# Low parts of split weights: a VectorE subtraction replaced by an accumulating DMA

## The chip, the core and the metric

The kernel runs on one core of one Trainium2 chip. The metric is device time in microseconds (us) of one execution; the time before is the median of three runs. The core has a matrix engine (TensorE; the profile writes PE for its products and PEld for its weight loads), VectorE (DVE), ScalarE (ACT), GpSimd (POOL) and SyncE (SP). Each takes its instructions strictly in its own order and waits on semaphores for the others. DMAs are issued from an engine's queue; before the change every DMA of the kernel is issued by SP.

## The reference

One layer on a sequence of 2048 positions and 1024 channels, all in float32: a LayerNorm, one wide projection, two branches (attention with 16 heads, and a causal convolution of 31 taps), each closed by a gate and a projection, then a gated merge, an output projection, a residual and a LayerNorm.

```python
h = x @ w_in                                     # 2048x1024 by 1024x9216
q, k, v, z_sb, c_val, c_gate, z_cv, g_sb, g_cv = jnp.split(h, SPLIT_POINTS, axis=-1)
o_sb = _stick_breaking_attention(q, k, v)
y_sb = (o_sb * silu(z_sb)) @ w_sb_proj
u = _causal_depthwise_conv(c_val * sigmoid(c_gate), conv_w, conv_b)
y_cv = (silu(_layer_norm(u, conv_ln_g, conv_ln_b)) * silu(z_cv)) @ w_cv_proj
merged = sigmoid(g_sb) * y_sb + sigmoid(g_cv) * y_cv
return _layer_norm(DEEPNORM_ALPHA * x + merged @ w_out, ln_g, ln_b)
```

## The kernel before

**Split products.** Every float32 matrix a is held as two tiles: hi, its value copied into the type float32r, and lo = a - hi. A product of two such matrices is three matmuls: hi by hi, hi by lo and lo by hi. The helper `split` (L112 to L114) makes the two parts: ACT copies the source into hi (L113), then DVE subtracts hi from the source into lo (L114). It serves the weights, the activations, and the attention weights of each head alike, so L113 and L114 stand for all of them in the profile; the tile names tell them apart: `whi`, `wlo` for weights, `xh`, `xl` for activations, `th`, `tl` for attention weights.

**The projection stream.** The projections are cut into blocks of 128 output columns, 176 of them; a block has two chunks of 512 positions, a chunk four pieces, a piece six matmuls of 128x512 (L194), so 24 matmuls a chunk and 48 a block. `load_w` (L141) brings the 1024x128 weights of a block: twice, for half of the contraction each, SP loads 256 KB into `wraw` (L148) and `split` makes `whi` and `wlo`. There are two `wraw` tiles, each of one half, and two pairs `whi`, `wlo`, each of a whole block: a new block's parts can be written when the block before the last one is used up. The load of the next block is emitted in the second piece of a block.

**Pairs.** At both ends of a run of eight blocks, and in a few other places, `pair` (L221) takes two blocks, a and b, crosswise: first chunk of a, first of b, second of a, second of b. So that one chunk's activations can load beside the other's products. Two of the weight loads there have a single chunk, 24 matmuls, between the moment at which their tiles come free and the moment at which they are needed: that of b, and that of the block after the pair.

**The weave.** TensorE's order is the order of emission. The attention (logits L572 and L573, sigmoid on ACT L575, running product on DVE L578 into `nb`, transposes L601, split into `th` and `tl`, product with the values L617) and the projection stream are woven into one list by estimated costs. The other engines' orders are made by the scheduler from priorities. The attention ends about 2660 us after the start; then come the attention branch's projection for the second half, an output projection (L900), the convolution branch's projection, and a last output projection. In these the blocks run without attention beside them.

**GpSimd** does little: some memsets, the power -0.5 and the products for the norms (L124, L119, one column each), and copies of single columns (L322 to L326, L377).

Of the kernel before, what the change touches and what calls it, by code (L numbers as in the profile page):

```python
# [8 lines left out]
F32 = mybir.dt.float32  # L9
F32R = mybir.dt.float32r  # L10
AF = mybir.ActivationFunctionType
ALU = mybir.AluOpType
# [13 lines left out]

# The weave: buffers of weights, the lead of the logits, and distances and paces in pieces of the projection stream.
NBW = 4
# [26 lines left out]
def layer_kernel(ctx: ExitStack, tc, x, w_in, w_sb, w_cv, w_out, vecs, cw, rows, out):  # L55
    """All sequences are reversed in time: row r is position S-1-r, so that a query r reads
    the keys s > r and the stick is broken in the direction of growing s.

    Every float32 product runs as float32r passes over an exact split a = hi + lo.

    The tensor engine runs in the order of emission: two streams, the attention and the
    projections, are woven so that what one waits for is covered by the other."""
    nc = tc.nc
# [28 lines left out]
    def dma(dst, src):  # L92
        """A copy of bytes: float32r has float32's bits."""
        nc.sync.dma_start(out=dst.bitcast(F32) if dst.dtype == F32R else dst,
                          in_=src.bitcast(F32) if src.dtype == F32R else src)
# [20 lines left out]
    def negmean(mr):  # L116
        """-mean * rstd"""
        nm = sm.tile([P, 1], F32, name="nm")
        nc.gpsimd.tensor_scalar(out=nm, in0=mr[:, 0:1], scalar1=mr[:, 1:2], scalar2=-1.0, op0=ALU.mult, op1=ALU.mult)  # L119
        return nm  # L120
# [18 lines left out]

    # -------------------------------------------------------------- projections, in pieces  # L140
    def load_w(src, col):  # L141
        """A block of 128 columns of a weight, [block, partition, kb, column], as hi and lo, contraction on the partitions."""
        hi = wp.tile([P, KB, P], F32R, name="whi", bufs=2)
        lo = wp.tile([P, KB, P], F32R, name="wlo", bufs=2)
        for g in range(2):
            ks = slice(g * 4, g * 4 + 4)
            raw = wp.tile([P, 4, P], F32, name="wraw", bufs=2)
            nc.sync.dma_start(out=raw, in_=src[col // P][:, ks])  # L148
            split(raw, hi[:, ks], lo[:, ks])
        return hi, lo  # L150

    class Fill:
        """The pieces of the projection stream: (cost in us of the tensor engine, emit)."""

# [20 lines left out]
        def parts(self, src, col, xs, use, *by):  # L175
            """A block: the pieces, per chunk, of out^T[col.., chunk] for each (chunk, acts) of xs; use(chunk, psum, ..) takes
            it, with what the loads `by` have brought. Also the item that loads the weights of the next block."""
            b = {"src": (src, col)}
            me = len(self.blocks)
            self.blocks.append(b)  # L180

            def chunk(c, acts):
                box = {}

                def piece(g):
                    if g == 0:
                        self.weights(me)
                        box["ps"] = mm_p.tile([P, CH], F32, name="mm")
                        box["by"] = [load(c) for load in by]
                    wh, wl = b["w"]  # L190
                    xh, xl = acts()
                    for kb in (2 * g, 2 * g + 1):
                        for n, (l, r) in enumerate(((wh, xh), (wh, xl), (wl, xh))):
                            nc.tensor.matmul(box["ps"], lhsT=l[:, kb], rhs=r[kb], start=(kb == 0 and n == 0),  # L194
                                             stop=(kb == KB - 1 and n == 2))
                    if g == 3:
                        with tc.high_priority(offset=500):
                            use(c, box["ps"], *box["by"])
                return [(1.3, lambda g=g: piece(g)) for g in range(4)]

            return [chunk(c, acts) for c, acts in xs], (0, lambda: self.weights(me + 1))
# [19 lines left out]
        def pair(self, one, two, first=(), freed=((), ())):  # L221
            """Two blocks, the first chunk of both before the second of either. The items `first` run beside these
            pieces, freed[n] as the activations of chunk n are used up."""
            (a, na), (b, nb) = self.parts(*one), self.parts(*two)
# [27 lines left out]
    def prep(c):  # L252
        """The normed input of chunk c, transposed and split, into xt[c], in pieces."""
        rows_ = []
# [28 lines left out]
    def xa_tile(to, key):  # L283
        """The next block of a chunk's activations, hi and lo."""
        t = [xa.tile([P, CH], F32R, name=n, bufs=2 * KB) for n in ("xh", "xl")]
        hi, lo = to.setdefault(key, ([], []))
        hi.append(t[0])
        lo.append(t[1])
        return t
# [65 lines left out]
    def even_odd(t):  # L355
        """A row kept as its even and then its odd positions, in the order of the positions."""
        return t.rearrange("p (e n) -> p n e", e=2)

    def block_u(F, m, h):
        """u = c_val * sigmoid(c_gate) of a block of channels."""  # L360
        sg = {}
# [21 lines left out]

    # -------------------------------------------------------------- causal depthwise convolution, norm over channels
    ysum = {}
    convs = []

    def conv(m, h, u):
        """y[r] = sum over d of t[d] u[r+d] + b, with t the taps reversed, on even and odd positions:
        y0 = t0 * (u0 - u1) + (t0 + t1) * u1,  y1 = t1 * (u0+ - u1) + (t0 + t1) * u1."""  # L390
        n = HN + H1
# [38 lines left out]
    def conv_mean(h):  # L430
        """The means over the channels of half h, as items."""
        def mean(c):
# [8 lines left out]
    def conv_ln(c):  # L441
        """The norm over the channels of chunk c, the swish and the gate of the branch, as items."""
        nb = CH // P
# [56 lines left out]

    # -------------------------------------------------------------- attention, in items
    def attention(at, kv, lg_p, pv_p):
        """Summed by parts: with E[r, s] the product of 1 - sigmoid over the keys after r up to s, the weight of s is
        E[r, s-1] - E[r, s], so that o[r] = v[r] + sum over s >= r of E[r, s] (v[s+1] - v[s]), with v[S] = 0."""
        dd = at.tile([P, HALF], F32, name="dd", bufs=1)
# [10 lines left out]
        def head(i, a, h):  # L516
            """The steps of head 2i+a for the queries of half h, each (L items, T/PV items)."""
            k2, v2, qd, ql = {}, {}, {}, {}
# [124 lines left out]
    def weave_attention(steps):  # L643
        """The steps as one list of (cost, emit): the logits run ahead of the transposes, those of the products."""
        ls = []
# [23 lines left out]

    # -------------------------------------------------------------- branch projections, output  # L670
    acts = {}

    def load_acts(key, src, c):
        """The activations of chunk c, split where they land, as items."""
        def load(m):
            hi, lo = xa_tile(acts, key)
            raw = st()
            dma(raw, src[c, m])
            split(raw, hi, lo)
        return [(0, lambda m=m: load(m)) for m in range(KB)]  # L680

    def branch(n, h):
        """A gated branch of the merge for half h: of the attention into pdr, of the convolution into mdr."""
        def gate(m):
# [28 lines left out]
    def run(F, blks, freed):  # L713
        """The blocks of a half, by pairs at both ends so that one chunk's activations load beside the other's products."""
        F.pair(*blks[:2])
# [26 lines left out]
    def newest():  # L742
        """The newest instruction of the vector engine."""
        return next((i for i in reversed(nc.cur_bb.bb.instructions) if i.engine == mybir.EngineType.DVE), None)
# [19 lines left out]

    # -------------------------------------------------------------- the main phase
    with ExitStack() as s2:
# [90 lines left out]

    # -------------------------------------------------------------- the rest
    with ExitStack() as s2:
# [20 lines left out]
        def output(F, c, freed):  # L880
            """The output projection of chunk c, the residual and the post-norm."""
            def unit(j, z, q, g, box):
# [92 lines left out]
```

## Time and profile before

| | |
|---|---|
| median of 3 runs (lowest, highest) | 3039.43 us (3039.3, 3042.27) |
| profiled execution, first to last instruction (its span) | 3036.5 us |
| lies around the span, by the median | 2.9 us |
| PE, PEld, DVE, ACT, POOL busy | 2959.8, 2484.1, 2381.6, 1269.5, 88.3 us |
| DMA moved | 455.92 MB, 16 engines 46.0% busy |
| granted TensorE clock, mean | 0.996 |

The profiled execution has no separate device time on record, only its span. In the profile a row of a timeline gives start, duration, engine, line, operation, output tile <- input tiles, and in brackets the idle time of that engine before it and what ended it. L194 means line 194 of the kernel before. Matmuls overlap in the records: a 128x512 matmul shows 0.39 us, though the next starts about 0.23 us after it.

### The profile page before, as it was taken

What the parts mean: (1) busy time and instruction counts of PE and PEld (TensorE: products, weight loads), DVE (VectorE), ACT (ScalarE), POOL (GpSimd) and SP (SyncE); (2) the same over time, 40 slices, a digit from 0 to 9 for tenths busy, and PEclk for the clock granted to TensorE, in tenths of its full rate; (3) what the DMA queues carried; (4) which work ended last, traced back from release to release, by engine and by line L of the source; (5) the groups of instructions that cost most, each with busy time, mean ns of one, the idle gap of its engine ahead of it and who ended that gap; (6) DMA issues with size and microseconds to landing.
All of it is one profiled execution on the core that took longest, in us unless ns stands there. A gap on an engine that the chain in (4) does not pass through costs nothing.

```text
span 3036.5 us, 41850 instructions
## 1 busy us (share of the span) xinstructions
PE 2959.8 (97%) x15304; PEld 2484.1 (82%) x15304; DVE 2381.6 (78%) x3175; ACT 1269.5 (42%) x2308; POOL 88.3 (3%) x178
## 2 busy tenths in 40 slices
PE   7999999999999999999999999999999999999998
PEld 6888888888887788888888888887888878878886
DVE  5587787777879888788879888879887788856656
ACT  5333333333336344444445444445445455533222
POOL 1000000000000000000000000000000000000000
PEclk9999999999999999999999999999999999999999
DMA  7543443434434533343335344335545666685552
GB/s 269 172 144 112 148 139 117 149 125 130 139 101 140 169 100 110 114 131 123 111 112 189 103 143 141 99 103 175 164 155 161 191 224 191 208 280 197 161 189 78
DMA packets 260221, 455.92 MB, mean 150 GB/s; under 512 B 30384, under 2 KB 55088, under 8 KB 259888
## 3 DMA queue, kind: packets, MB, share of 16 engines
q1 hardware_dynamic: 260016, 453.25, 46.0%
q8 instruction: 120, 1.97, 0.3%
q14 instruction: 85, 0.70, 0.1%
HBM read 292.70 MB, written 160.43 MB: 149 GB/s over the span
## 4 chain that ended last, share of the span: by engine, by line
PE 73%; DVE 11%; issue 10%; DMA 3%; ACT 2%; POOL 1%; SPq 0%; DVEq 0%; POOLq 0%; ACTq 0%
PE mm L194 52%; PE pv L617 7%; PE tp L601 6%; DVE nb L578 3%; PE lg L573 3%; PE lg L572 3%; DVE tl L114 2%; DVE wlo L114 1%; DVE cy L402 1%; PE mo L900 1%; DMA st<-ydq 1%; DMA ydq<-st 1%; DVE xl L114 1%; DVE st L494 0%; DVE st L493 0%
## 5 line engine op out<-in xcount | busy, mean ns | idle before, releaser
L194 PE MATMUL mm<-xh,whi 128*128 128x512 f32 x2816 | 1144.5, 406 | 1.7 <-ACT whi L113 1.5
L194 PE MATMUL mm<-xh,wlo 128*128 128x512 f32 x2816 | 1110.1, 394 | 1.4 <-DVE wlo L114 1.4
L194 PE MATMUL mm<-xl,whi 128*128 128x512 f32 x2816 | 1106.2, 393 | 1.2 <-DVE xl L114 1.2
L194 PEld LDWEIGHTS mm<-xh,wlo 128*128 128x128 f32 x2816 | 530.0, 188 | 120.9 <-DVE wlo L114 1.9
L194 PEld LDWEIGHTS mm<-xl,whi 128*128 128x128 f32 x2816 | 532.9, 189 | 86.8 <-DVE xl L114 2.4
L194 PEld LDWEIGHTS mm<-xh,whi 128*128 128x128 f32 x2816 | 531.5, 189 | 86.4 <-ACT whi L113 1.9
L113 ACT ACTIVATE th<-tp 128x512 fp32r<-128x512 f32 (+1 forms) x576 | 329.4, 572 | 613.9 <-PE tp L601 606.1
L114 DVE TENSOR_TENSOR tl<-tp,th 128x512 fp32r<-128x512 f32 (+1 forms) x576 | 376.5, 654 | 180.1 <-ACT th L113 178.2
L575 ACT ACTIVATE nb<-lg 128x512 f32<-128x512 f32 (+3 forms) x640 | 334.9, 532 | 308.9 <-PE lg L573 299.0
L578 DVE TENSOR_TENSOR_SCAN nb<-nb,dd 128x256 f32<-128x256 f32 (+7 forms) x256 | 345.1, 1350 | 42.2 <-ACT nb L575 41.5
L601 PE MATMUL tp<-ident,nb 128*128 128x128 f32 x2176 | 337.8, 274 | 20.3 <-DVE nb L578 18.2
L578 DVE TENSOR_TENSOR_SCAN nb<-nb,zero 128x1024 f32<-128x1024 f32 x128 | 300.0, 2346 | 36.5 <-ACT nb L575 36.2
L601 PEld LDWEIGHTS tp<-ident,nb 128*128 128x128 f32 x2176 | 263.4, 140 | 77.9 <-DVE nb L578 22.5
L113 ACT ACTIVATE whi<-wraw 128x512 fp32r<-128x512 f32 x352 | 217.6, 629 | 261.1 <-PE mm L194 238.8
L617 PE MATMUL pv<-tl,v 128*128 128x256 f32 (+1 forms) x1152 | 292.1, 282 | 12.2 <-DVE tl L114 11.6
L114 DVE TENSOR_TENSOR wlo<-wraw,whi 128x512 fp32r<-128x512 f32 x352 | 237.4, 682 | 80.0 <-ACT whi L113 52.9
L617 PE MATMUL pv<-th,v 128*128 128x256 f32 (+1 forms) x1152 | 299.5, 281 | 0.0
L572 PE MATMUL lg<-k,qd 128*128 128x512 f32 (+3 forms) x640 | 246.4, 386 | 11.6 <-ACT nb L575 7.0
L617 PEld LDWEIGHTS pv<-tl,v 128*128 128x128 f32 x1152 | 218.1, 189 | 36.4 <-DVE tl L114 17.2
L573 PE MATMUL lg<-k,ql 128*128 128x512 f32 (+3 forms) x640 | 233.7, 366 | 0.0
L617 PEld LDWEIGHTS pv<-th,v 128*128 128x128 f32 x1152 | 217.8, 189 | 18.5 <-issue 0.2
L402 DVE SCALAR_TENSOR_TENSOR cy<-cu,csum,cy 128x512 f32<-128x512 f32 x240 | 178.1, 742 | 4.4 <-ACT cy L398 0.9
(107 smaller groups left out, 2460.0 us busy)
## 6 DMA issues: line engine op xcount, KB each, us to landing
wraw<-in_w_in SPq DMA_DIRECT2D x288, 256.0 KB, 3.2
k<-kdr SPq DMA_DIRECT2D x192, 128.0 KB, 2.9
v<-vdr SPq DMA_DIRECT2D x96, 256.0 KB, 3.5
kdr<-st SPq DMA_DIRECT2D x64, 256.0 KB, 2.1
qdr<-st SPq DMA_DIRECT2D x64, 256.0 KB, 2.2
qd<-qdr SPq DMA_DIRECT2D x128, 128.0 KB, 2.8
vdr<-st SPq DMA_DIRECT2D x64, 256.0 KB, 2.0
xr<-in_x SPq DMA_DIRECT2D x32, 256.0 KB, 3.8
```

Of the source, the lines that this page charges most:

```text
L113: nc.scalar.activation(hi, src, AF.Copy)
L114: nc.vector.tensor_tensor(out=lo, in0=src, in1=hi.bitcast(F32), op=ALU.subtract)
L194: nc.tensor.matmul(box["ps"], lhsT=l[:, kb], rhs=r[kb], start=(kb == 0 and n == 0), stop=(kb == KB - 1 and n == 2))
L402: nc.vector.scalar_tensor_tensor(out=dst, in0=src[:, j:j + HN], scalar=t, in1=first, op0=ALU.mult, op1=ALU.add)
L572: nc.tensor.matmul(lg[:, :w], lhsT=qd[c][:, js], rhs=k2[kc][:, ko:ko + w], start=True, stop=False)
L573: nc.tensor.matmul(lg[:, :w], lhsT=ql[c][:, js], rhs=k2[kc][:, ko:ko + w], start=False, stop=True)
L575: nc.scalar.activation(nb[:, o:o + w], lg[:, :w], AF.Sigmoid, scale=-QS)
L578: nc.vector.tensor_tensor_scan(out=nb[:, :w], data0=nb[:, :w], data1=dd[:, :w] if diag else zero.to_broadcast([P, w]), initial=0.0 if diag ...
L601: nc.tensor.transpose(out=tp[:, at_:at_ + P], in_=tiles[j][:, so:so + P], identity=ident)
L617: nc.tensor.matmul(o[:, :w], lhsT=lv, rhs=tt[:, o0:o0 + w], start=(diag and t == 0 and n == 0 and e == 0), stop=(last and t == nt - 1 and ...
L900: nc.tensor.matmul(ps, lhsT=a[kb][:, js], rhs=b[:, kb, qs], start=(kb == 0 and n == 0), stop=(kb == KB - 1 and n == 2))
```

## The change

In `load_w` alone, the raw weights are still loaded into `wraw` and copied into `whi` by ACT. Then ACT copies `whi` with scale -1 into `wlo`, and a DMA issued by GpSimd reads the same 256 KB of weights from memory once more and adds them to what stands in `wlo`. DVE no longer takes part. The other callers of `split` are as they were. Lines below the change stand two lower than before (L194 becomes L196).

```diff
             raw = wp.tile([P, 4, P], F32, name="wraw", bufs=2)
             nc.sync.dma_start(out=raw, in_=src[col // P][:, ks])
-            split(raw, hi[:, ks], lo[:, ks])
+            nc.scalar.activation(hi[:, ks], raw, AF.Copy)
+            nc.scalar.activation(lo[:, ks], hi[:, ks].bitcast(F32), AF.Copy, scale=-1.0)
+            nc.gpsimd.dma_start(out=lo[:, ks], in_=src[col // P][:, ks].bitcast(F32R), accum_op=ALU.add)
```

It takes 352 instructions from DVE and adds 352 to ACT and 352 DMAs to GpSimd's queue. A `wraw` tile is now free once ACT has read it. The third product of a block on TensorE waits for the DMA instead of DVE; TensorE's order is the same, row by row.

On GpSimd at the start of the program, before: the powers and products of the norm of the input's rows (`mrs`, `nm`), then the single columns of the first value block (`st`, `vnext`).

```order
L124 TENSOR_TENSOR mrs<-mrs,mhalf 128x1
L119 TENSOR_SCALAR nm<-mrs 128x1
L124 TENSOR_TENSOR mrs<-mrs,mhalf 128x1
L119 TENSOR_SCALAR nm<-mrs 128x1
L124 TENSOR_TENSOR mrs<-mrs,mhalf 128x1
L119 TENSOR_SCALAR nm<-mrs 128x1
L124 TENSOR_TENSOR mrs<-mrs,mhalf 128x1
L119 TENSOR_SCALAR nm<-mrs 128x1
L322 TENSOR_SCALAR st<-st 128x1
```

The same place now, with the accumulating DMAs of line 151.

```order
L124 TENSOR_TENSOR mrs<-mrs,mhalf 128x1
L119 TENSOR_SCALAR nm<-mrs 128x1
L151 DMA wlo<-in_w_in 128x512
L124 TENSOR_TENSOR mrs<-mrs,mhalf 128x1
L119 TENSOR_SCALAR nm<-mrs 128x1
L151 DMA wlo<-in_w_in 128x512 x2
L124 TENSOR_TENSOR mrs<-mrs,mhalf 128x1
L119 TENSOR_SCALAR nm<-mrs 128x1
L124 TENSOR_TENSOR mrs<-mrs,mhalf 128x1
L119 TENSOR_SCALAR nm<-mrs 128x1
L151 DMA wlo<-in_w_in 128x512 x5
L324 TENSOR_SCALAR st<-st 128x1
```

The first half of block 0 stands behind the norm of the fifth group of rows, the second half of block 0 and the first of block 1 behind the sixth, the second of block 1 behind the eighth.

On ACT where the attention has ended and the last phase begins, before: the parts of the two blocks of a pair (`whi`), between activations (`xh`) and the output weights (`woh`).

```order
L113 ACTIVATE whi<-wraw 128x512 x2
L113 ACTIVATE xh<-st 128x512 x3
L113 ACTIVATE woh<-raw 128x1024 x3
L113 ACTIVATE xh<-st 128x512 x5
L113 ACTIVATE whi<-wraw 128x512
L113 ACTIVATE xh<-st 128x512
L113 ACTIVATE whi<-wraw 128x512
L113 ACTIVATE xh<-st 128x512 x3
```

The same place now.

```order
L149 ACTIVATE whi<-wraw 128x512 x2
L113 ACTIVATE xh<-st 128x512
L150 ACTIVATE wlo<-whi 128x512
L113 ACTIVATE xh<-st 128x512
L150 ACTIVATE wlo<-whi 128x512
L113 ACTIVATE woh<-raw 128x1024
L113 ACTIVATE xh<-st 128x512
L113 ACTIVATE woh<-raw 128x1024
L149 ACTIVATE whi<-wraw 128x512
L113 ACTIVATE woh<-raw 128x1024
L113 ACTIVATE xh<-st 128x512 x3
L150 ACTIVATE wlo<-whi 128x512
```

The copies of block a of the pair stand together before and have an `xh` between them and each negation now. The first copy of block b has moved ahead of the last `woh` and three `xh`, and its negation stands behind these.

## Prediction

> **What bounds the kernel now.** I read the page first, for the busy times.
>
> ```profile
> span 3036.5 us, 41850 instructions
> PE 2959.8 (97%) x15304; PEld 2484.1 (82%) x15304; DVE 2381.6 (78%) x3175; ACT 1269.5 (42%) x2308; POOL 88.3 (3%) x178
> ```
>
> PE is busy 97% of the span, but matmul records overlap, so this alone doesn't say that PE is at its pace. The timeline of PE does:
>
> ```profile
> 1500.55 0.39 PE L194 MATMUL mm<-xh,whi 128*128 128x512 f32 x1
> 1500.78 0.40 PE L194 MATMUL mm<-xl,whi 128*128 128x512 f32 x1
> 1501.01 0.39 PE L194 MATMUL mm<-xh,wlo 128*128 128x512 f32 x1
> ```
>
> One product starts every 0.23 us, with no gap, in the middle of the weave. TensorE sets the time; what DVE saves is worth only the moments at which TensorE waits for DVE. The waits of TensorE's weight loads name them (total, times, longest):
>
> ```profile
> PEld tp L601 <- DVE nb L578: 22.5, 18, 3.5
> PEld pv L617 <- DVE tl L114: 17.2, 21, 2.2
> PEld tp L275 <- DVE xr L266: 13.1, 4, 12.3
> PEld lg L572 <- ACT nb L575: 10.7, 11, 2.6
> PEld tp L601 <- DVE tl L114: 3.8, 7, 0.8
> PEld mm L194 <- DVE wlo L114: 1.9, 1, 1.9
> ```
>
> The 13.1 us for `xr` are the first transposes of the program, which wait for the input. The other four rows with DVE make 22.5 + 17.2 + 3.8 + 1.9 = 45.4 us: no relief of DVE can bring more, out of 3036.5. The weights' low part itself is waited for once.
>
> **What is removed.** The groups by line price the subtraction and the copy beside it:
>
> ```profile
> L113 ACT ACTIVATE whi<-wraw 128x512 fp32r<-128x512 f32 x352 | 217.6, 629 | 261.1 <-PE mm L194 238.8
> L114 DVE TENSOR_TENSOR wlo<-wraw,whi 128x512 fp32r<-128x512 f32 x352 | 237.4, 682 | 80.0 <-ACT whi L113 52.9
> ```
>
> DVE loses 237.4 us, nearly all of it beside TensorE's work. How tight DVE is, stage by stage (length, then busy time of PE, PEld, DVE, ACT and POOL, clock, DMA share, GB/s):
>
> ```profile
> 60.00:900.00 840.00, 837.82 (x4246) 702.46 (x4245) 641.29 (x895) 305.94 (x592) 28.39 (x54) 1.00 0.42 136
> 1100.00:2300.00 1200.00, 1182.71 (x6364) 999.27 (x6363) 1005.20 (x1251) 529.67 (x981) 17.73 (x26) 1.00 0.41 130
> 2300.00:2680.00 380.00, 360.59 (x1970) 305.92 (x1969) 317.88 (x403) 200.63 (x360) 2.03 (x2) 0.99 0.64 204
> ```
>
> Up to 900 us TensorE loses 2 us in 840: nothing to gain. From 1100 to 2680 DVE is busy 84%. The subtractions are 237.4 / 3036.5 = 8% of the time, so 84% becomes 76%. If waiting in a queue goes as load over idle share, 0.84/0.16 = 5.2 becomes 0.76/0.24 = 3.2, 40% less. On the 43.5 us behind `nb` and `tl` that is 17 us, and the 1.9 us go too. The form of this rule is my assumption; the bounds are 0 and 45.4.
>
> **What is added on ACT.** 352 negations, which no row has; the copy beside them, 629 ns, is the nearest, with a start 0.52 us after the one before where two stand together (whi x2 in 1.16 us, below). That is 220 us, and ACT goes from 42% to 49%. Between 1100 and 2300 us its 530 / 1200 = 44% becomes 51%, load over idle share from 0.8 to 1.05, a third more. On the 10.7 us that TensorE waits for ACT this is 3.5 us. The splits `th`, whose lateness DVE's `tl` inherits, I put at as much again: 7 us. So the balance of the engines is 17 + 2 - 7 = 12 us gained; I take 10.
>
> **What is added as DMA.** 352 transfers of 256 KB more. Nothing issued by POOL, and no accumulation, is in this trace. The rows nearest to it (issue to landing, us), and the slowest kind of POOL operation (ns, minimum/median/maximum):
>
> ```profile
> kdr<-st SPq DMA_DIRECT2D x64, 256.0 KB, 2.1
> wraw<-in_w_in SPq DMA_DIRECT2D x288, 256.0 KB, 3.2
> wraw<-in_w_sb SPq DMA_DIRECT2D x32, 256.0 KB, 4.2
> raw<-in_w_out SPq DMA_DIRECT2D x8, 512.0 KB, 6.0
> L124 POOL TENSOR_TENSOR var<-var,mhalf x4: 1007/1241/1465, 1478.3 to 2571.4; 128x4 f32<-128x4 f32 x4
> ```
>
> From below: a load like any other, 3.2 us. From above: it moves its bytes twice, like the 512 KB load, 6.0, with some of the crowd of the last phase and a POOL operation for the issue, 8 us in all. I take the last phase's plain load and one such operation, 4.2 + 1.2 = 5.4 us from the end of the negation to the landing; call it X. The Trainium skill, "DMA: Bandwidth & Descriptors", section "Anatomy of one DMA — SWDGE (gpsimd) path", fits 2.0 us plus the bytes at 436 GB/s for a DMA from GpSimd, an estimated 2.6 us here; by it the shortfalls of 1.2 us below are gone. The trace's plain loads take longer than that, so I don't lower X.
>
> Does TensorE wait for X? A block's tiles come free one block ahead of its use. With attention woven in, a block lasts some 17 us (3036.5 / 176), and X plus the copies passes unseen. The short places are the pairs, where 24 products at 0.23 us, 5.5 us, are all there is. One in the last phase, on ACT and then PE:
>
> ```profile
> 2866.23 1.16 ACT L113 ACTIVATE whi<-wraw 128x512 fp32r<-128x512 f32 x2 [7.67 <-PE mm L194]
> ...
> 2872.15 0.39 PE L194 MATMUL mm<-xh,wlo 128*128 128x512 f32 x1
> ```
>
> ACT waits for the tile, copies both halves until 2867.39, and the low part is needed at 2872.15. Now the first negation ends at about 2867.9, and 4.2 us are left: X = 5.4 is 1.2 us late. The code has six such places after the attention (a pair at each end of the two runs, less the two loads that the output projection covers). Three are like this one: 3.6 us. At the first, an `xh` stands between copy and negation: 1.2 + 0.5 = 1.7. The other two are later on ACT:
>
> ```profile
> 2671.51 0.43 SPq L148 DMA_DIRECT2D wraw<-in_w_sb  x1
> ...
> 2676.20 0.63 ACT L113 ACTIVATE whi<-wraw 128x512 fp32r<-128x512 f32 x1
> 2690.88 1.14 ACT L113 ACTIVATE whi<-wraw 128x512 fp32r<-128x512 f32 x2
> ...
> 2679.05 0.50 PE L194 MATMUL mm<-xh,wlo 128*128 128x512 f32 x1 [1.43 <-DVE wlo L114]
> 2695.50 0.39 PE L194 MATMUL mm<-xh,wlo 128*128 128x512 f32 x1
> ```
>
> The block of 2695.50: 2690.88 + 1.14 + 0.5 + 5.4 = 2697.9, 2.4 us late. The block of 2679.05 already waits. Its first copy now stands ahead of a `woh` and three `xh`, its negation behind them. If SP loads at 2671.51 as before, the raw weights are there at 2675.7, the copy ends at 2676.2, and 1 + 3 x 0.55 + 0.5 later, at 2679.4, the negation; landing 2684.8, 5.7 us late. If SP, no longer held by DVE, loads 3 us earlier, it is 2.8 us; I take 4.5. The last phase: 3.6 + 1.7 + 2.4 + 4.5 = 12 us. At X = 8 it is 2.6 us more at each of six places, 28 us; at X = 3.2 only the fifth is left, about 2.
>
> **The start.**
>
> ```profile
> 14.82 0.33 SPq L148 DMA_DIRECT2D wraw<-in_w_in  x1
> ...
> 15.23 0.61 ACT L113 ACTIVATE whi<-wraw 128x512 fp32r<-128x512 f32 x1
> 15.75 1.43 ACT L278 ACTIVATE st<-tp,vec 128x512 f32<-128x512 f32 x2
> ...
> 17.44 0.59 POOL L119 TENSOR_SCALAR nm<-mrs 128x1 f32<-128x1 f32 x1
> ...
> 20.87 0.63 PE L194 MATMUL mm<-xh,wlo 128*128 128x512 f32 x1
> ```
>
> Ahead of the `st` of 15.75 ACT now has one negation, two copies and two negations more or less together, of which the second copy needs the third raw load. That load waited for DVE until 14.82 and now waits only for ACT; with 3 to 5 us to land it is there at about 16.5, so `st` comes near 18, 2.3 us later, and TensorE's first product with it. POOL issues the first accumulation behind the `nm` that ends at 18.0; 18.0 + 5.4 = 23.4, against 20.87 + 2.3 = 23.2. The next block's is behind one more norm, which waits for its rows, and adds 1.5; the block after this pair, a short place as above, 1. Start: 2.3 + 0.2 + 1.5 + 1 = 5 us, between 2 and 9.
>
> **Crowding.** 92 MB on 456 MB, a fifth more. In 2300 to 2680 us the DMA engines' 0.64 goes to some 0.75, and the loads of activations there come later: 3 us, between 0 and 8. POOL's single columns for `st` now queue behind accumulations that wait for ACT. POOL had waited long for its inputs there, and a few us hide; nothing.
>
> Sum: 5 + 12 + 3 - 10 = +10 us on the span of 3036.5, 3046.5; with the 2.9 us around it, 3049.5 against the median of 3039.43, 0.33% slower. About 0.2%, 6 us, is what a measurement of this kernel tells from no change.
>
> **The rivals.**
> - *DVE's relief decides (faster).* X stays under the 4.2 us of slack, so the last phase costs 2 us, the start 3, crowding 0, and the queue rule holds in full with little harm from ACT: 5 - 18 = -13, 3026. For it: plain loads take 3.2 us, and DVE is the engine TensorE waits for most. Against: the last phase's loads take 4.2.
> - *A slow accumulation.* X is 8 us or more: start 9, last phase 28, the woven pairs, with some 8 us of lead, 8 more, crowding 7, less 10: +42, 3081. A way to it: each issue on POOL is held by the DVE instruction then running, up to 2.35 us for the longest running products below, so X = 5.4 + 2.35 = 7.75.
>
> ```profile
> L578 DVE TENSOR_TENSOR_SCAN nb<-nb,zero 128x1024 f32<-128x1024 f32 x128 | 300.0, 2346 | 36.5 <-ACT nb L575 36.2
> ```
>
> The Trainium skill, "SBUF — State Buffer", section "SBUF: two separate sides", has this as the "DVE blocks DMA" trap: GpSimd can't write descriptors while DVE holds their shared port in a two-port mode. No run here shows it yet; by the 0.23 us pace of the products it would show only in pairs.
> - *Nothing measurable.* The same terms with X near 4.2: 3 + 6 + 1 - 10 = 0, 3039.
> - *The change not doing what it says* is no rival for DVE, whose rows are gone from the order; but the raw load stays, so it saves no transfer.
>
> **How the numbers follow.** Forecast 0.38 (+6 to +30 us), slow accumulation 0.13, nothing measurable 0.25, relief 0.24. So faster 0.24, same 0.25, slower 0.51. The range leaves out a tenth on each side: 3022, near the relief's largest gain less the unavoidable start, to 3082, the slow accumulation as priced.
>
> **What would show it.** Right: DVE near 2144 us, ACT near 1490; waits of PE for a DMA into `wlo` at the start and at the six places, 1 to 5 us each; `nb` and `tl` waits down by a third. Landings of `wlo` near 5 us from issue. Wrong: landings under 4 us with no wait on `wlo`; or over 8, with waits on `wlo` all over the weave; or `nb` and `tl` waits as large as before or larger, which would say that ACT has taken over DVE's part.

## The result and the profile after

| | before | changed |
|---|---|---|
| median of the runs, us (lowest, highest) | 3040.22 (3039.3, 3042.27), 4 runs | 3123.52 (3120.13, 3127.55), 4 runs |
| ratio, 95% interval | | 1.0276 [1.0263, 1.0289] |
| profiled execution: device time, span | no time, 3036.5 | 3127.55, 3125.8 |
| mean granted TensorE clock | 0.996 | 0.983 |

The changed kernel is 83 us, 2.8%, slower (84 us against the 3039.43 us on record before; below it is called 84). The direction was forecast, the size was not: 10 us forecast, 3082 the upper end. The page of the changed kernel (engines; then the DMA queues, with packets, MB and share of 16 engines):

```profile
span 3125.8 us, 42335 instructions
...
PE 2998.6 (96%) x15304; PEld 2507.3 (80%) x15304; DVE 2183.0 (70%) x2823; ACT 1447.3 (46%) x2660; POOL 389.7 (12%) x530
...
q1 hardware_dynamic: 260016, 453.25, 45.2%
q0 software_dynamic: 50688, 92.30, 17.9%
```

DVE is relieved, ACT loaded, as the change says. The last row is GpSimd's queue: 92 MB take 17.9% of the engines, where SP's 453 MB take 45.2%. Per megabyte that is 0.194% against 0.0997%, twice as much.

The waits of TensorE's weight loads, changed kernel:

```profile
PEld tp L603 <- DVE nb L580: 33.5, 19, 4.4
PEld mm L196 <- DMA wlo<-in_w_sb: 19.3, 5, 7.2
PEld lg L574 <- ACT nb L577: 18.6, 13, 3.8
PEld pv L619 <- DVE tl L114: 18.3, 30, 1.7
...
PEld mm L196 <- DMA wlo<-in_w_cv: 6.7, 2, 3.4
PEld mm L196 <- DMA wlo<-in_w_in: 5.9, 3, 3.0
PEld pv L619 <- ACT th L113: 5.8, 6, 2.7
```

Two things stand in it. TensorE waits for accumulations, 31.9 us in ten waits. And the attention's waits for DVE and ACT, which the relief was to shorten, have grown: `nb` behind DVE from 22.5 to 33.5, behind ACT from 10.7 to 18.6, and `th` from 0.2 to 5.8.

Four stages of it (start and end, length, busy PE, PEld, DVE, ACT, POOL, clock, DMA share, GB/s):

```profile
62.00:930.00 868.00, 861.41 (x4364) 721.18 (x4362) 585.34 (x794) 378.23 (x730) 131.59 (x177) 1.00 0.65 173
...
1100.00:2300.00 1200.00, 1177.67 (x6279) 993.61 (x6278) 913.54 (x1095) 590.95 (x1104) 133.31 (x163) 0.99 0.59 158
2300.00:2730.00 430.00, 395.75 (x2099) 332.51 (x2098) 314.04 (x382) 228.03 (x416) 37.20 (x42) 0.96 0.71 206
2730.00:2780.00 50.00, 38.71 (x135) 30.31 (x136) 15.94 (x21) 17.64 (x27) 5.22 (x6) 0.80 0.84 262
```

From 62 to 930 us TensorE is idle for only 7 us, with as much traffic as anywhere behind the start in the program's first half. Between 1100 and 2300 us it starts 85 products fewer than before in the same time, some 16 us at the pace before. Most of the time is lost after that, in the end of the attention and in the last phase, above all its first pairs, and there the granted clock is 0.96 and 0.80. What the clock does behind a wait, on the timeline of PE:

```profile
2761.24 0.39 PE L196 MATMUL mm<-xl,whi 128*128 128x512 f32 x1
2768.42 0.79 PE L196 MATMUL mm<-xh,wlo 128*128 128x512 f32 x1 [6.79 <-DMA wlo<-in_w_sb]
...
2769.44 0.63 PE L196 MATMUL mm<-xl,whi 128*128 128x512 f32 x1
2769.86 0.63 PE L196 MATMUL mm<-xh,wlo 128*128 128x512 f32 x1
...
2774.40 0.39 PE L196 MATMUL mm<-xl,whi 128*128 128x512 f32 x1
2774.63 0.40 PE L196 MATMUL mm<-xh,wlo 128*128 128x512 f32 x1
```

After the wait of 6.79 us products start 0.43 us apart instead of 0.23, until 2774: 13 of them, 2.6 us more that no wait names. The same stands behind a wait of 2.98 us that ends at 2730.5. The Trainium skill, "TensorE: Matmul & The Clock Gate", section "Part 1: The HAM clock gate", says that idleness puts the clock at half and that activity is judged in windows of 3.4 us; the 5.7 us of slow products here agree with a return after one or two of these.

The landings (KB each, median us from issue), which the prediction had at 5.4 us from the end of the negation:

```profile
wlo<-in_w_in POOLq DMA_DIRECT2D x288, 256.0 KB, 6.2
...
wlo<-in_w_sb POOLq DMA_DIRECT2D x32, 256.0 KB, 7.3
...
wlo<-in_w_cv POOLq DMA_DIRECT2D x32, 256.0 KB, 7.0
```

### The profile page after: what moved, and what is told of

Same layout as the page of the kernel before. It is cut to its first block, busy times and chain, and to the rows that moved or that the text cites. A ratio compares the mean times of both kernels' runs of the same rounds, so it can differ in the third digit from the quotient of the medians.

```text
span 3125.8 us, 42335 instructions
## 1 busy us (share of the span) xinstructions
PE 2998.6 (96%) x15304; PEld 2507.3 (80%) x15304; DVE 2183.0 (70%) x2823; ACT 1447.3 (46%) x2660; POOL 389.7 (12%) x530
## 3 DMA queue, kind: packets, MB, share of 16 engines
q1 hardware_dynamic: 260016, 453.25, 45.2%
q0 software_dynamic: 50688, 92.30, 17.9%
## 5 line engine op out<-in xcount | busy, mean ns | idle before, releaser
L196 PE MATMUL mm<-xh,whi 128*128 128x512 f32 x2816 | 1154.5, 410 | 0.8 <-DVE st L114 0.5
L196 PE MATMUL mm<-xh,wlo 128*128 128x512 f32 x2816 | 1120.1, 398 | 27.4 <-DMA wlo<-in_w_sb 17.2
L196 PE MATMUL mm<-xl,whi 128*128 128x512 f32 x2816 | 1115.7, 396 | 2.2 <-DVE xl L114 2.2
L196 PEld LDWEIGHTS mm<-xh,wlo 128*128 128x128 f32 x2816 | 535.6, 190 | 152.8 <-DMA wlo<-in_w_sb 19.3
L196 PEld LDWEIGHTS mm<-xl,whi 128*128 128x128 f32 x2816 | 538.5, 191 | 90.1 <-DVE xl L114 3.9
L196 PEld LDWEIGHTS mm<-xh,whi 128*128 128x128 f32 x2816 | 537.5, 191 | 86.8 <-DVE st L114 1.0
L151 POOL DMA_DIRECT2D wlo<-in_w_in x288 | 251.1, 891 | 1616.3 <-ACT wlo L150 1265.5
L603 PEld LDWEIGHTS tp<-ident,nb 128*128 128x128 f32 x2176 | 265.9, 141 | 91.5 <-DVE nb L580 33.5
L150 ACT ACTIVATE wlo<-whi 128x512 fp32r<-128x512 f32 x352 | 218.0, 629 | 2.4
```

Of the source, the lines that this page charges most:

```text
L150: nc.scalar.activation(lo[:, ks], hi[:, ks].bitcast(F32), AF.Copy, scale=-1.0)
L151: nc.gpsimd.dma_start(out=lo[:, ks], in_=src[col // P][:, ks].bitcast(F32R), accum_op=ALU.add)
L603: nc.tensor.transpose(out=tp[:, at_:at_ + P], in_=tiles[j][:, so:so + P], identity=ident)
```

## The experiments

Four costs could make the 84 us: less relief than thought, ACT's negations, the new traffic, and the waits for it. The first runs add them one by one. Each time is a median beside its own runs of before (3038.6 to 3040.4).

**Relief alone.**

```diff
             nc.scalar.activation(hi[:, ks], raw, AF.Copy)
-            ...negation, accumulating DMA
-        return hi, lo
+        return hi, hi
```

> The low parts of the weights aren't made at all: neither subtraction, negation nor accumulation; the third product reads the high part in their place. So DVE loses its 352 subtractions and nothing is added. If the relief of DVE is worth what the prediction said (17 to 19 us of waits), 3020 to 3030 us. If it is worth nothing because the attention's waits have another cause, 3037 to 3043.

3025.1 us, ratio 0.9947 [0.9930, 0.9964]: 14 us gained. The relief is real, and this is all there is of it. TensorE's waits behind `nb` and `tl`, to be read against 22.5, 17.2, 10.7 and 3.8 before:

```profile
PEld tp L600 <- DVE nb L577: 20.5, 15, 2.7
PEld pv L616 <- DVE tl L114: 13.8, 22, 1.7
...
PEld lg L571 <- ACT nb L574: 8.4, 12, 1.9
PEld tp L600 <- DVE tl L114: 4.9, 7, 1.9
```

Some 4 us less behind DVE and 2 less behind ACT. Of the 8 us besides, 1.9 are the low part's wait, and some 5 are products that took less time: PE is busy 2955.2 us for the same 15304 products, where it was 2959.8.

**Relief and the negations.**

```diff
             nc.scalar.activation(lo[:, ks], hi[:, ks].bitcast(F32), AF.Copy, scale=-1.0)
-            nc.gpsimd.dma_start(out=lo[:, ks], in_=..., accum_op=ALU.add)
         return hi, lo
```

> The accumulating DMA is left out; the low part is the negated high part that ACT writes. DVE is relieved, ACT has the 352 negations, TensorE waits for no DMA. Theory that ACT's added work makes the attention stage worse: 25 to 45 us over the run with the relief alone. Theory that the extra DMA traffic does it: within 10 us of the run with the relief alone.

3034.9 us, 0.9981 [0.9972, 0.9991]. The negations cost 10 us of the 14, with TensorE's wait for ACT's `nb` up from 8.4 to 12.6. That is less than the theory of ACT needs.

**The negations without the relief.** As the run before, and in the place of the DMA:

```diff
+            nc.vector.tensor_tensor(out=lo[:, ks], in0=raw, in1=lo[:, ks].bitcast(F32), op=ALU.add)
```

> No accumulating DMA: ACT negates, and DVE adds the raw weights to the negation, so DVE has as many operations as before and ACT 352 more. Theory that ACT's added work costs: 25 us or more over before, 3065. Theory that traffic and waits cost, not ACT: within 10 us of before, 3030 to 3050.

3053.0 us, 1.0040 [1.0025, 1.0055], 14 us over before: between the two expectations. ACT's part is 10 to 14 us, whether DVE is relieved or not.

**All the work, but nobody waits for it.**

```diff
-        return hi, lo
+        return hi, hi
```

> All of the change's work is done, negation and accumulating DMA, but the third product reads the high part, so TensorE never waits for an accumulation. The change took 84 us. Theory that waits for the accumulations at the start and in the pairs, with the half clock behind each, make 45 us: about 3078. Theory that the traffic itself is what costs in the attention stage: 30 us or more over the run without the DMA. Theory that ACT does it: within 10 us of the run without the DMA.

3088.0 us, 1.0158 [1.0143, 1.0173]: 53 us over the run without the DMA. The traffic costs more than all else, though TensorE doesn't read what it brings. The last 35 us come when TensorE does read it, as waits and what follows them. So the theory of waits alone (3078) falls short, and that of ACT falls. How it costs, first in the landings of the others, without the DMA and then with it:

```profile
k<-kdr SPq DMA_DIRECT2D x192, 128.0 KB, 2.8
...
wraw<-in_w_sb SPq DMA_DIRECT2D x32, 256.0 KB, 4.1
st<-asb SPq DMA_DIRECT2D x32, 256.0 KB, 3.5
```

```profile
k<-kdr SPq DMA_DIRECT2D x192, 128.0 KB, 3.7
...
wraw<-in_w_sb SPq DMA_DIRECT2D x32, 256.0 KB, 5.7
st<-asb SPq DMA_DIRECT2D x32, 256.0 KB, 4.6
```

These land 0.9 to 1.6 us later, though not all do: the raw weights of `in_w_in` go from 3.1 to 3.4 us. Then in the waits of ACT, without and with:

```profile
ACT st L459 <- DMA ydq<-st: 33.3, 18, 4.7
...
ACT xh L113 <- DMA st<-asb: 4.0, 6, 1.2
```

```profile
ACT st L460 <- DMA ydq<-st: 55.5, 19, 5.5
...
ACT xh L113 <- DMA st<-asb: 17.6, 15, 4.0
```

All waits of ACT for transfers together go from 116 to 195 us. ACT takes its instructions in order: while it waits for a late transfer of `st`, what stands behind it waits too, the attention's sigmoids `nb` and splits `th` among it, then DVE's running products and splits, and TensorE behind both. That path is pieced together from the waits at its two ends; TensorE's end, without and with:

```profile
PEld tp L602 <- DVE nb L579: 21.1, 17, 3.0
...
PEld lg L573 <- ACT nb L576: 12.6, 12, 3.6
PEld pv L618 <- DVE tl L114: 10.2, 17, 1.6
```

```profile
PEld tp L603 <- DVE nb L580: 32.5, 18, 3.5
PEld pv L619 <- DVE tl L114: 20.6, 28, 1.8
PEld lg L574 <- ACT nb L577: 17.7, 15, 3.8
```

These three rows grow by 27 us. The stage in which convolution norms and activations are loaded beside the attention, without and with:

```profile
2300.00:2680.00 380.00, 360.99 (x1976) 304.73 (x1975) 297.93 (x368) 219.90 (x399) 2.03 (x2) 1.00 0.64 205
```

```profile
2300.00:2680.00 380.00, 347.60 (x1847) 291.12 (x1846) 281.49 (x339) 203.84 (x374) 31.82 (x36) 0.96 0.71 207
```

In the same 380 us TensorE now starts 1847 products instead of 1976, 7% fewer, with a granted clock of 0.96 instead of 1.00. The bytes per second are about the same, 207 against 205, with the accumulations among them.

**A sixteenth of the bytes.** Is it the bytes, or the 352 issues on GpSimd and what queues behind them?

```diff
-            nc.gpsimd.dma_start(out=lo[:, ks], in_=src[col // P][:, ks]...
+            nc.gpsimd.dma_start(out=lo[:, 4 * g, :32], in_=src[col // P][:, 4 * g, :32]...
```

> As the run whose accumulation is unread, but each accumulating DMA moves 128 bytes a partition, a sixteenth, so the low part is left negated but for that piece, and the third product reads the high part. Count, order and waits of GpSimd's queue stay. Without the DMA the kernel took 3035, with it 3088. Theory that the bytes crowd the other transfers: near 3035 to 3045. Theory that the issues on GpSimd, or what queues behind them, cost: 3075 or more.

3034.9 us, 0.9988 [0.9978, 0.9998], the time without any DMA, though the third product reads the high part here too. So as many issues and packets cost nothing; the bytes do.

```profile
q0 software_dynamic: 50688, 5.79, 3.4%
```

**A plain copy of the same bytes.**

```diff
-            nc.gpsimd.dma_start(out=lo[:, ks], in_=src[col // P][:, ks].bitcast(F32R), accum_op=ALU.add)
+            nc.gpsimd.dma_start(out=lo[:, ks].bitcast(F32), in_=src[col // P][:, ks])
```

> As the run whose accumulation is unread, but GpSimd's DMA writes the raw weights over the negation in place of adding; the third product reads the high part. Same bytes from memory, no reading of the destination. In the changed kernel an accumulated megabyte takes the DMA engines twice as long as any other (17.9% of them for 92 MB, 45.2% for 453). Theory that the engines' time is what crowds: the cost over 3035 halves, 3055 to 3065, and the landing falls from 6.1 to about 4.5 us. Theory that bytes from memory crowd: 3080 or more.

3058.2 us, 1.0064 [1.0047, 1.0081]: 23 us over the run without the DMA, against 53 for the accumulation.

```profile
q0 software_dynamic: 28160, 92.30, 9.8%
...
wlo<-in_w_in POOLq DMA_DIRECT2D x288, 256.0 KB, 4.5
```

The share of the engines is 9.8%, against 18.4% for the accumulation in the unread run, and the cost falls with it, from 53 to 23 us, while the bytes from memory are the same. The median landings of the other transfers hardly tell the two apart (`k` 3.5 us, `st` from `asb` 4.5, `wraw` of `in_w_sb` 5.2); ACT's waits for transfers do, 160 us in all against 195, where it was 116 without the DMA and 128 with a sixteenth of the bytes. The copy differs from the accumulation in its type as well, float32 where that has float32r, so which of the two makes the price is not shown.

**Added from SBUF.**

```diff
-            nc.gpsimd.dma_start(out=lo[:, ks], in_=src[col // P][:, ks].bitcast(F32R), accum_op=ALU.add)
+            nc.gpsimd.dma_start(out=lo[:, ks], in_=raw.bitcast(F32R), accum_op=ALU.add)
```

> As the run whose accumulation is unread (3088), but the DMA adds the raw weights from the tile in SBUF into which SP has loaded them, so 92 MB less is read from memory; the third product reads the high part. Theory that the DMA engines' time crowds the other transfers: 3070 or more, with about the same share of the engines. Theory that reads from memory crowd: 3060 or less. The raw tile is held until the accumulation lands, which may cost some us of its own.

3108.4 us, 1.0231 [1.0215, 1.0247]. With 92 MB less read from memory and nearly the same share of the engines, 17.5%, it is 20 us slower than the run that reads memory. That is the first theory's side of the expectation, but the waits of SP say that the run doesn't test it:

```profile
SPq L148 <- DMA wlo<-wraw: 909.4, 321, 14.0
```

SP, in order too, stands 909 us waiting for raw tiles that the accumulation holds, where it had stood 276 us for ACT, so other loads are issued late. Once issued they land sooner than in the unread run, `wraw` of `in_w_sb` after 3.1 us instead of 5.7 and `k` after 3.2 instead of 3.7. So this run decides neither way; that the reads from memory alone don't set the cost rests on the plain copy.

**Halves.** The waits for accumulations, by giving them more lead and changing nothing else:

```diff
-        hi = wp.tile([P, KB, P], F32R, name="whi", bufs=2)
-        lo = wp.tile([P, KB, P], F32R, name="wlo", bufs=2)
+        hi, lo = [], []
         for g in range(2):
+            hi.append(wp.tile([P, 4, P], F32R, name=f"whi{g}", bufs=2))
+            lo.append(wp.tile([P, 4, P], F32R, name=f"wlo{g}", bufs=2))
...
```

> The changed kernel, with the parts of a block held in two tiles of half the contraction each, in the same space. A half comes free 12 products earlier or is needed 12 later, so a pair leaves 8 us in place of 5.5. Nothing else is changed. Theory that the 35 us between the unread run and the changed kernel are waits for the accumulations with too short a lead: the waits on it after the start vanish, 3090 to 3100. If these 35 us come of something else: 3115 or more.

3085.3 us, 1.0149 [1.0134, 1.0164]: 38 us less than the changed kernel, more than the 24 to 34 expected. The waits for accumulations are not gone, as they were expected to be after the start, but less than half:

```profile
PEld mm L197 <- DMA wlo<-in_w_sb: 9.3, 3, 6.3
...
PEld mm L197 <- DMA wlo<-in_w_in: 3.3, 3, 1.9
...
PEld mm L197 <- DMA wlo<-in_w_cv: 1.8, 3, 1.0
```

Between the two profiled executions PE has 25 us less idle time and 22 us less busy time for the same products. So the pace comes back with the waits gone.

**Halves in the kernel before**, the control.

> The kernel before, with VectorE's subtraction, and the parts of a block in two tiles of half the contraction each: the control for the run of the changed kernel with halves, which came out 38 us faster than the changed kernel. Theory that halves only take away waits for the accumulations: within 6 us of before, which waits for a low part once. If halves help by themselves, for instance because ACT's copies wait less for tiles: 3030 or less, and that much of the 38 us is not the accumulation's.

3033.0 us, 0.9984 [0.9976, 0.9993], 6 us less than before: at the border of the first expectation. So some 32 of the 38 us are the accumulation's. This kernel computes the whole layer and is, by a little, faster than the kernel before.

**The subtraction on GpSimd**, another way to the relief:

```diff
+            nc.gpsimd.tensor_tensor(out=lo[:, ks], in0=raw, in1=hi[:, ks].bitcast(F32), op=ALU.subtract)
```

> GpSimd subtracts the high part from the raw weights in place of DVE: no negation on ACT, no second transfer, DVE relieved. If relief alone is worth 14 us and GpSimd's slower subtraction (my estimate from its small operations is about 1.5 us) is hidden by the lead of a block: 3022 to 3030, faster than before. If it hinders DVE's operations through something they share, DVE's mean durations grow and it is 3040 or more.

3077.7 us, 1.0126 [1.0109, 1.0143]: 53 us over the relief alone, with no more traffic than before, and TensorE waits for GpSimd's `wlo` only once, 1.7 us. DVE is busy 2332.7 us here and 2182.3 with the relief alone, for the same 2823 instructions. A split and a convolution tap on DVE before, then GpSimd's subtraction and the same two in this run:

```profile
L114 DVE TENSOR_TENSOR tl<-tp,th 128x512 fp32r<-128x512 f32 (+1 forms) x576 | 376.5, 654 | 180.1 <-ACT th L113 178.2
...
L402 DVE SCALAR_TENSOR_TENSOR cy<-cu,csum,cy 128x512 f32<-128x512 f32 x240 | 178.1, 742 | 4.4 <-ACT cy L398 0.9 <-issue 0.3
```

```profile
L150 POOL TENSOR_TENSOR wlo<-wraw,whi 128x512 fp32r<-128x512 f32 x352 | 531.9, 1521 | 2075.9 <-ACT whi L149 1873.7 <-PE lg L574 41.2 <-PE tp L602 38.8
L114 DVE TENSOR_TENSOR tl<-tp,th 128x512 fp32r<-128x512 f32 (+1 forms) x576 | 376.9, 654 | 229.7 <-ACT th L113 228.0
...
L403 DVE SCALAR_TENSOR_TENSOR cy<-cu,csum,cy 128x512 f32<-128x512 f32 x240 | 198.1, 825 | 9.9 <-ACT cy L399 6.7
```

The tap, with two inputs in SBUF, grows from 742 to 825 ns; `tl`, whose one input is in PSUM, stays at 654. The Trainium skill, "SBUF — State Buffer", section "Who interferes with whom", has this rule, that such an instruction contends with GpSimd's reads; the rows agree. That DVE's longer instructions make all of the 53 us is argued from these rows, not shown by a run.

**Early and late.** The change in blocks 3 to 59 alone, and in blocks 60 to 175 alone, with `split` as before in the others:

```diff
+        loaded[0] += 1
...
+            if not (3 <= loaded[0] < 60):
+                split(raw, hi[:, ks], lo[:, ks])
+                continue
```

> The change in blocks 3 to 59 alone, which run in the first 900 us; the other blocks as before. There VectorE has slack, and TensorE lost 2 us in 840 before and 7 in 868 in the changed kernel. Theory that crowding and short leads cost only where nothing is left to hide them: within 6 us of before, 3033 to 3045. Theory that traffic costs in proportion to its bytes, 84 us x 57/176: about 3066.

> The change in blocks 60 to 175 alone, from about 900 us to the end; the first 60 as before. Theory that nearly all of the cost lies there but for some 8 us at the start: 3110 to 3120. Theory of cost in proportion to bytes, 84 us x 116/176: about 3094.

Early: 3042.0 us, 1.0007 [0.9997, 1.0017], no measurable change. Late: 3108.0 us, 1.0221 [1.0201, 1.0240], 68 us. A third of the accumulations costs 1.5 us, as the theory of slack has it, not in proportion to bytes. Late came out a little below its expectation: with blocks 0 to 2, the start, some 15 us of the 84 are left over, where TensorE is idle for 7 us more than before in the first 60. The other 8 are not settled.

## Why the prediction was right and wrong

| term | forecast | measured | run that shows it |
|---|---|---|---|
| relief of DVE | -19 | -14 | relief alone |
| negations on ACT | +7 | +10 (+14 without the relief) | relief and negations |
| crowding by the traffic, slow products included | +3, up to 8 | +53 | unread |
| waits for accumulations, start and pairs, with the slow products behind them | +17 | +35 | changed against unread |
| sum | +10 (with the balance taken as -10) | +84 | |

*The bound* was right: TensorE sets the time, and relief of DVE has a ceiling, 45.4 us, of which 14 were to be had. That 14 came near 19 is in part luck. The queue rule gave 17 us off the 43.5 behind `nb` and `tl`; in the relief alone they fell by 4, and the rest came from ACT's waits, from the low part's and from the pace of the products, which the sum didn't have.

*The balance of DVE and ACT* was right in sign, and too good: -4 for -10. ACT's negations eat most of what the relief gives, since TensorE waits for ACT and DVE in one chain.

*The waits* were found near where they were forecast: two at the start and one of 0.5 us later in the rows of w_in, then five of w_sb and two of w_cv after the attention, where six were counted; ten in all, 31.9 us. The size was off by the landing, 7.0 to 7.3 us from the issue in the last phase where X was 5.4 from the end of the negation, the upper end being 8. X = 8 had priced them at 28 + 9. In the profiled executions the step from unread to the changed kernel is 41 us, 23 of them idle time of PE and 18 slower products.

*Crowding* is the step that failed: "the loads of activations there come later: 3 us, between 0 and 8". The share of the engines was foreseen, 0.75, and came to 0.71. What wasn't asked is who stands behind a late load. An in-order ACT does, with the attention's sigmoids and splits behind it, in a stage where TensorE waits for them already. The price of an accumulated megabyte, twice that of a copied one, was not in the sum either: 30 of the 53 us, by the plain copy. The prediction had named waits for `nb` and `tl` as large as before as a sign that ACT has taken over DVE's part. The sign came, but its reading was wrong: with ACT's negations and no DMA these waits stay at 21.1 and 10.2 us, and the traffic brings them to 32.5 and 20.6.

*The clock* is the second step that failed: the sum has no term for it. A long wait can be followed by products at half pace, as the timeline above shows with 2.6 us behind one of 6.79 us. Over the run the mean clock fell from 0.996 to 0.983. The pages give the size: for the same 15304 products PE is busy 2959.8 us before and 2998.6 in the changed kernel, 39 us more, and idle for 50 us more, which makes the 89 us between the two spans. Without the DMA PE is busy 2960.2 us, in the unread run 2980.5. So of the 52 us that crowding adds to the span, 32 are idle time and 20 slower products. No run has the waits without the slower products, so these are a share of each cost and not a cost beside them.

*The rivals.* The slow accumulation was nearest, X being close to its 7.75, but it too came to only 3081 for want of the crowding. The way to it that was named, issues held back by DVE's running instruction, isn't seen. The issues on GpSimd in the changed kernel (minimum, median, maximum):

```profile
L151 POOL DMA_DIRECT2D wlo<-in_w_in x288: 856/865/1247, 16.9 to 2338.0; - x144
```

The median is 9 ns above the fastest, beside a DVE that is busy 70% of the time. By the Trainium skill, "SBUF — State Buffer", section "SBUF: two separate sides", the hold comes of two-port modes; these rows show none.

*DVE and ACT busy* came to 2183 and 1447 where 2144 and 1490 were forecast: neighbouring instructions overlap in the records by about 0.1 us, so busy time falls and grows by less than the sum of durations. The relief alone takes 199.3 us off DVE, not 237.4.

## What to carry to other kernels

Moving work off an engine that isn't the bound is worth at most the waits for it and the slower products behind these; a kernel that leaves the work out measures that first, here 14 us. A transfer that nobody waits for still has a price where the engines that read the others work in order and the bounding engine waits for them already; ask what stands behind the load that comes late. Where a transfer takes the place of an instruction, count the shortest lead between its tile coming free and being needed, not the mean one.

## What was not expected of the hardware

- An accumulating DMA takes the DMA engines about twice a plain one of the same bytes: 18.4% against 9.8% for 92.30 MB, with 50,688 packets against 28,160, and lands after 6.1 us where the plain one took 4.5. The plain one was float32, the accumulation float32r.
- The pace of TensorE's products halved for 5.7 us behind a wait of 6.79 us. Mostly by such stretches PE's busy time grew by 39 us for the same products.
- GpSimd's subtraction of 128x512 took 1.52 us in the mean, and slowed DVE's taps by 11%, but not its instructions with an input in PSUM.
